# A sparse-attention stage whose index scores move from VectorE to TensorE

## The chip, the cores and the metric

The kernel runs on one core of one Trainium2 chip. The metric is the device time of one execution in microseconds; of several executions the median counts. TensorE (PE) multiplies matrices, VectorE (DVE), ScalarE (ACT) and GpSimd (POOL) work on tiles, SyncE (SP) issues most of the DMA transfers. Each engine works through its own list of instructions in the order in which the program wrote them, and waits on semaphores for the others.

## The reference

The program is two transformer blocks; the change lies in one stage of the second, the sparse attention (`dsa_attention`). For 512 tokens with 1,024 features, a small index network scores every earlier token for every token (8 index heads of 64 features), the best 128 are kept, and 16 heads of latent attention run over those alone. Cut to what matters:

```
h = x @ w_in                                   # 456 columns: c_q 256, c_kv 128, k_idx 64, w_idx 8
c_q, c_kv = rms_norm(c_q, g), rms_norm(c_kv, g)
q_idx = (c_q @ w_qidx).reshape(S, 8, 64)
k_idx = layer_norm(k_idx, g, b)
s_idx = einsum('thd,sd->ths', q_idx, k_idx)
score = einsum('ths,th->ts', relu(s_idx), w_idx * scale)     # sum over 8 index heads
score = where(key_pos <= t_pos, score, -inf)
_, sel = top_k(score, 128)
logits = einsum('thc,tkc->thk', q_abs, c_kv[sel]) * qk_scale + bias[t5_bucket(dist)]
o = softmax(logits) @ c_kv[sel] @ w_uv @ w_o
```

## The kernel before

Weights are float32. `WStream` loads them in slabs of 128 x 2048 and splits each into a high part (`wh`, a cast on ACT, L295) and a low part (`wl`, a subtraction on DVE or POOL, L302); a product is then three matmuls (`mm3`: high times high, L307, and the two mixed ones, L308 and L309). `ws.get()` hands out the next slab and splits so many further ones as `ws.ahead` says.

The stage is `dsa_in` (L2487), then `dsa_att`. No scheduler moves anything: the order of the calls is the order on every engine. Tokens come in four tiles of 128. `dsa_in` does the following.

- For each tile t, `gemm_n` makes the 512 columns of `x @ w_in` (24 matmuls, two slabs). For t = 0 and 1, `flip` turns the input tile that is needed two steps later (`xth`, `xtl`).
- `norm(t)` copies the result (`hs`, ACT), squares it for the norms, and after its first `yield` scales it (8 small DVE instructions with three square roots on ACT between them). `wi` holds the head weights.
- `turn(t)` transposes `hs` on PE (L2538), applies the gains (`df`, 4 DVE instructions) and splits into `ch` (ACT) and `cl` (DVE).
- `index_q(w, half)` makes the index queries of two tiles (24 matmuls of 256 columns, `xth`), `value` the attention values of a tile.
- `scores(i)` makes the scores of the rows of tile i against the 128 (i + 1) keys up to it: for each of 8 heads three matmuls, a Relu on ACT (L2567), and on DVE a multiplication by the head's weight that is added to `sco` (L2569, L2571); at the end a minimum with the causal mask (L2574). Tile 0 needs no selection.
- `select()` is a generator of DVE instructions. For one tile it takes 16 rounds, each a MAX (L2587: the eight largest) and a MATCH_REPLACE (L2589: strike them out), then an `is_equal` and a scaling into the mask `negm`. It runs tile 1, with tile 2 beside it once that is scored, and then tile 3. `step(n)` advances it by n steps; `scores(i, n)` takes n steps after each head.
- `make(h)` projects queries and keys of attention head h (9 matmuls, 2 ACT and 2 DVE instructions). Three heads are made ahead, with 8 steps after each; then the attention loop starts. It goes over heads for tiles 0 to 2 first, projects three heads ahead, and takes on the average 2.25 steps of the selection of tile 3 per iteration until that is done.

`dsa_in` sets `ws.lo_eng = "pool"` at its start, so that POOL makes the low parts. Before it, two constants are made on DVE: `identb` (L2473) and `negm[0]` (L2501).

Of the kernel before, what the change touches and what calls it, by code (L numbers as in the profile page):

```python
# [9 lines left out]
F32 = mybir.dt.float32  # L10
# [3 lines left out]
AF = mybir.ActivationFunctionType  # L14
OP = mybir.AluOpType
# [8 lines left out]
KT = D // 128  # L24
# [252 lines left out]
class Builder:  # L277
# [40 lines left out]
            if between and k % 2:  # L318
                between()

    def gemm_n(self, slabs, xh, xl, t0, ps):

        kk = 0
        n = 4 * len(slabs)
        for s in slabs:
            h = s[0].rearrange("p (k c) -> p k c", k=4)
            l = s[1].rearrange("p (k c) -> p k c", k=4)
            for k in range(4):
                self.mm3(ps, (xh[:, kk, t0:t0 + 128], xl[:, kk, t0:t0 + 128]), (h[:, k], l[:, k]), kk == 0, kk == n - 1)
                kk += 1  # L330
# [2131 lines left out]
    def phase_dsa(self):  # L2462
        nc, A, ws = self.nc, self.A, self.ws
        V, G, S_ = nc.vector, nc.gpsimd, nc.scalar
        dt = self.dram.tile
        self.d_dq = dt([16, 128, 2, 128], F32, name="d_dq")
        self.d_dk = dt([16, 128, 512], F32, name="d_dk")
        with ExitStack() as c:
            op_ = c.enter_context(self.pool(name="da_o", bufs=1))
            vs = op_.tile([128, 4, 1024], F32, name="vs")  # L2470
            negm = [op_.tile([128, 128 * (i + 1)], BF16, name=f"negm{i}") for i in range(4)]
            identb = op_.tile([128, 128], BF16, name="identb")
            V.tensor_copy(identb, self.ident)  # L2473
            with ExitStack() as c1:
                with ExitStack() as c2:
                    self.acc_pool(c2)
                    bg, load = self.dsa_in(c1, vs, negm, c2.enter_context(self.pool(name="da_pt", bufs=4, space=PSUM)))
                self.dsa_att(c1, vs, negm, identb, load, bg)
            self.acc_pool(c, 8)
            self.ln_gains(c, 2)  # L2480
            ws.ahead = 0
            self.last_gemm(lambda k, t: (self.xth[:, k, t * 128:(t + 1) * 128], self.xtl[:, k, t * 128:(t + 1) * 128]),
                           [ws.get() for _ in range(4)], KT, self.acc, "acc", DN_ALPHA)
            ws.ahead = 2
            ws.hi_eng, ws.lo_eng = "act", "dve"

    def dsa_in(self, c, vs, negm, pt):  # L2487

        nc, A, ws = self.nc, self.A, self.ws
# [8 lines left out]
        caus = vs[:, 3, 256:384]  # L2498
        nc.scalar.dma_start(out=caus, in_=A["causal"][:, 0:128])
        nc.scalar.dma_start(out=wrk[0][:, 0:128], in_=A["causal"][:, 128:256])  # L2500
        V.tensor_scalar(negm[0], wrk[0][:, 0:128], -1.0, None, op0=OP.mult)  # L2501
        sp = c.enter_context(self.pool(name="da_s", bufs=1))
        c1 = ExitStack()
        tp = c1.enter_context(self.pool(name="da_t", bufs=3))
# [11 lines left out]
        def norm(t, ps):  # L2516
            h, s = hs[t], ss[:, t]
            S_.copy(h, ps)
            S_.activation(jk, ps[:, 0:256], AF.Square, accum_out=s[:, 0:1], scale=1.0 / 16)
            S_.activation(jk[:, 0:128], ps[:, 256:384], AF.Square, accum_out=s[:, 1:2])  # L2520
            yield
            V.bn_stats(st[:, t], h[:, 384:448])
            V.bn_aggr(s[:, 6:8], st[:, t])
            V.tensor_scalar(wi[:, t], h[:, 448:456], 8 ** -0.5 * 64 ** -0.5, None, op0=OP.mult)
            S_.activation(s[:, 2:3], s[:, 0:1], AF.Sqrt, bias=self.eps_col(1e-6), scale=1.0)
            S_.activation(s[:, 3:4], s[:, 1:2], AF.Sqrt, bias=self.eps_col(1e-6), scale=1.0 / 128)
            S_.activation(s[:, 4:5], s[:, 7:8], AF.Sqrt, bias=self.eps_col(1e-5), scale=1.0)
            V.reciprocal(s[:, 2:5], s[:, 2:5])
            V.tensor_scalar(h[:, 448:512], h[:, 384:448], s[:, 6:7], s[:, 4:5], op0=OP.subtract, op1=OP.mult)
            V.tensor_scalar(h[:, 384:448], h[:, 384:448], s[:, 6:7], s[:, 4:5], op0=OP.subtract, op1=OP.mult)  # L2530
            V.tensor_scalar(h[:, 256:384], h[:, 256:384], s[:, 3:4], None, op0=OP.mult)
            V.tensor_scalar(h[:, 0:256], h[:, 0:256], s[:, 2:3], None, op0=OP.mult)
            yield
# [12 lines left out]
        def index_q(w, half):  # L2546
            e = slice(256 * half, 256 * half + 256)
            for j in range(4):
                ps = acc()
                for k in range(2):  # L2550
                    cs = slice(k * 512 + j * 128, k * 512 + j * 128 + 128)
                    self.mm3(ps[:, 0:256], (w[0][:, cs], w[1][:, cs]), (ch[:, k, e], cl[:, k, e]), k == 0, k == 1)
                self.split(ps[:, 0:256], iqh[:, j, e], iql[:, j, e])

        def step(n):
            for _ in range(n):
                next(bg, None)

        def scores(i, steps=0):
            n = 128 * (i + 1)  # L2560
            sc = ip.tile([128, n], F32, name=f"sco{i}")
            for h in range(8):
                j, r = h // 2, slice(64 * (h % 2), 64 * (h % 2) + 64)
                ps = acc()
                self.mm3(ps[:, 0:n], (iqh[r, j, tsl[i]], iql[r, j, tsl[i]]), (ch[r, 3, 0:n], cl[r, 3, 0:n]), True, True)
                f = tp.tile([128, 512], F32, name="df", tag="df")
                S_.activation(f[:, 0:n], ps[:, 0:n], AF.Relu)  # L2567
                if h == 0:
                    V.tensor_scalar(sc, f[:, 0:n], wi[:, i, h:h + 1], None, op0=OP.mult)  # L2569
                else:  # L2570
                    V.scalar_tensor_tensor(sc, f[:, 0:n], wi[:, i, h:h + 1], sc, op0=OP.mult, op1=OP.add)  # L2571
                step(steps)
                yield
            V.tensor_tensor(sc[:, n - 128:], sc[:, n - 128:], caus, op=OP.min)  # L2574
            sco[i] = sc

        ready = []
# [1 line left out]
        def select():  # L2579

            started = []

            def rounds(i):
                n, a = 128 * (i + 1), i % 2
                src, wk = sco[i], wrk[a if i < 3 else 0][:, 0:n]
                for r in range(16):
                    V.max(m8[:, a], src)  # L2587
                    yield
                    V.match_replace(wk, m8[:, a], src, -3.3e38)  # L2589
                    src = wk  # L2590
                    yield
                V.tensor_tensor(wk, wk, sco[i], op=OP.is_equal)
                yield
                V.tensor_scalar(negm[i], wk, 1.0e30, None, op0=OP.mult)
                ready.append(i)
            both = [rounds(1)]
            while both:
                for g in list(both):
                    if next(g, both) is both:
                        both.remove(g)  # L2600
                if sco[2] is not None and not started:
                    started.append(rounds(2))
                    both += started
                yield
            yield from rounds(3)

        def value(w, t):
            for half in range(2):
                ps = acc()
                cs = slice(1024 + half * 512, 1536 + half * 512)  # L2610
                self.mm3(ps, (ch[:, 2, tsl[t]], cl[:, 2, tsl[t]]), (w[0][:, cs], w[1][:, cs]), True, True)
                S_.copy(vs[:, t, half * 512:(half + 1) * 512], ps)
# [40 lines left out]
        def make(h):  # L2653
            made[h] = proj(h)

        ws.lo_eng = "pool"
        slabs = [ws.get(), ws.get()]
        for t in range(4):
            ps = acc()
            self.gemm_n(slabs, self.xth, self.xtl, t * 128, ps)  # L2660
            if t < 2:
                self.flip(t + 2, pt, "dpt")
            if t == 2:
                turn(0)
                turn(1)
                ws.ahead = 1
                wq = ws.get()
            nm = norm(t, ps)
            next(nm)
            if t < 3:  # L2670
                next(nm)
        index_q(wq, 0)
        turn(2)
        next(nm)
        value(wq, 0)
        for _ in scores(1):
            pass
        bg = select()
        turn(3)
        for t in range(1, 3):  # L2680
            value(wq, t)
            step(3)
        ws.ahead = 0
        wk = ws.get()
        c2.close()
        qp = c.enter_context(self.pool(name="db_q", bufs=3, side="right"))
        index_q(wq, 1)
        for _ in scores(2, 1):
            pass
        wu = [ws.get(), ws.get()]  # L2690
        for _ in scores(3, 4):
            pass
        for h in range(3):
            make(h)
            step(8)
# [132 lines left out]
```

## Time and profile before

| | |
|---|---|
| median of 3 executions | 3916.84 us (3914.33 to 3918.34) |
| profiled execution | 3919.22 us, span 3917.4 us |
| mean granted TensorE clock | 0.975 of full speed |
| busy share of the span | PE 95%, DVE 60%, ACT 38%, POOL 25% |
| chain that ended last | PE 76%, DVE 11%, DMA 6%, ACT 3% |

The span is the time from the first to the last instruction of the profiled execution, whose own time is 1.8 us longer. PE is busy for 95% of it, and where it isn't, another engine is late. In the 40 slices of the page, PE falls below nine tenths only in few; one of them is the stage above, which begins in the trace at 3259.55 us and hands over to the attention loop at about 3378 us. Such a stage is read from its own waits, not from the shares of the whole.

### The profile page before, as it was taken

Reading aid. Unit: us, or ns where it says so; the run is one execution under the profiler, and the core shown is the slowest. Engines: PE = TensorE matmul, PEld = TensorE weight load, DVE = VectorE, ACT = ScalarE, POOL = GpSimd, SP = SyncE. Lnnn points to the kernel's source line nnn. Section 1 sums busy time; section 2 is a strip of 40 time slices with the busy share of each in tenths; the row PEclk is TensorE's granted clock in tenths of the full one; section 3 lists DMA queues with packets and bytes.
Section 4 is the critical chain, followed back from the end, with each engine's and each line's share of the span. In section 5 each row is a group of like instructions: output and inputs, shape, how many; then the busy total and the mean of one; then the engine's idle time right before and its main releaser. Section 6 shows DMA issues by size and latency. Waiting matters only on the chain.

```text
span 3917.4 us, 49840 instructions
## 1 busy us (share of the span) xinstructions
PE 3709.7 (95%) x19451; PEld 3039.8 (78%) x19456; DVE 2330.9 (60%) x4013; ACT 1499.9 (38%) x2159; POOL 997.5 (25%) x574
## 2 busy tenths in 40 slices
PE   8999799999999999999999998898889998699999
PEld 4788667788888878888888886787778886588887
DVE  3564265596999963444434437783665548846455
ACT  3322275553544543322322324663333324443232
POOL 1201053325433431211211214752421001112010
PEclk9999899999999999999999999999999999799999
DMA  6374554324455566655655643469735222252221
GB/s 250 124 277 160 161 152 144 110 76 131 176 178 178 184 198 174 164 147 157 160 148 160 164 129 110 143 179 268 190 119 155 85 96 77 83 185 97 97 105 57
DMA packets 483964, 582.32 MB, mean 149 GB/s; under 512 B 337904, under 2 KB 379760, under 8 KB 446096
## 3 DMA queue, kind: packets, MB, share of 16 engines
q1 hardware_dynamic: 479552, 571.20, 47.9%
q10 hardware_dynamic: 4176, 7.93, 0.6%
q8 instruction: 153, 2.51, 0.3%
q14 instruction: 83, 0.68, 0.1%
HBM read 456.37 MB, written 121.63 MB: 148 GB/s over the span
## 4 chain that ended last, share of the span: by engine, by line
PE 76%; DVE 11%; DMA 6%; ACT 3%; POOL 2%; issue 2%; SPq 1%; ACTq 0%; DVEq 0%; POOLq 0%
PE acc L307 14%; PE acc L309 13%; PE acc L308 13%; PE pv L309 8%; PE pv L308 8%; PE pv L307 8%; PE psc L1520 3%; DMA d_k<-ql 1%; DMA d_q<-ql 1%; PE dpo L2760 1%; POOL wl L302 1%; PE pz L2071 1%; DVE ob L1532 1%; PE acc L644 1%; DVE st L961 1%
## 5 line engine op out<-in xcount | busy, mean ns | idle before, releaser
L295 ACT CAST wh<-wr 128x2048 fp32r<-128x2048 f32 (+2 forms) x310 | 510.2, 1664 | 398.0 <-PE pv L309 291.7
L302 DVE TENSOR_TENSOR wl<-wr,wh 128x2048 fp32r<-128x2048 f32 (+2 forms) x203 | 461.2, 2291 | 154.5 <-ACT wh L295 154.3
L307 PE MATMUL pv<-wh,ah 128*128 128x512 f32 x1376 | 538.0, 391 | 9.7 <-ACT wh L295 9.7
L308 PE MATMUL pv<-wl,ah 128*128 128x512 f32 x1376 | 537.0, 390 | 1.5 <-DVE wl L302 1.5
L309 PE MATMUL pv<-wh,al 128*128 128x512 f32 x1376 | 537.1, 390 | 0.0
L302 POOL TENSOR_TENSOR wl<-wr,wh 128x2048 fp32r<-128x2048 f32 (+1 forms) x113 | 387.3, 3440 | 540.7 <-ACT wh L295 505.7
L307 PE MATMUL acc<-h2h,wh 128*128 128x512 f32 x1024 | 412.9, 403 | 0.0
L309 PE MATMUL acc<-h2h,wl 128*128 128x512 f32 x1024 | 402.9, 393 | 0.0
L308 PE MATMUL acc<-h2l,wh 128*128 128x512 f32 x1024 | 399.2, 390 | 0.0
L307 PEld LDWEIGHTS pv<-wh,ah 128*128 128x128 f32 x1376 | 259.4, 188 | 64.1 <-ACT wh L295 10.2
L308 PEld LDWEIGHTS pv<-wl,ah 128*128 128x128 f32 x1376 | 259.1, 188 | 56.2 <-DVE wl L302 2.0
L309 PEld LDWEIGHTS pv<-wh,al 128*128 128x128 f32 x1376 | 259.1, 188 | 54.6
L307 PE MATMUL acc<-xth,wh 128*128 128x512 f32 (+1 forms) x768 | 287.4, 374 | 0.7 <-ACT xth L295 0.7
L309 PE MATMUL acc<-xth,wl 128*128 128x512 f32 (+1 forms) x768 | 286.8, 373 | 0.0
L308 PE MATMUL acc<-xtl,wh 128*128 128x512 f32 (+1 forms) x768 | 284.8, 371 | 1.1 <-DVE xtl L302 1.1
L1371 DVE TENSOR_TENSOR py<-py,pv 128x512 f32<-128x512 f32 x119 | 80.4, 685 | 323.7 <-PE pv L309 323.7
L1532 DVE TENSOR_SCALAR ob<-iota,ttt 128x128 f32<-128x128 f32 x512 | 238.3, 527 | 0.0
L309 PEld LDWEIGHTS acc<-h2h,wl 128*128 128x128 f32 x1024 | 192.1, 188 | 43.2
L1521 ACT COPY gs<-psc 128x512 f32<-128x512 f32 x128 | 143.4, 1120 | 210.5 <-PE psc L1520 207.2
L308 PEld LDWEIGHTS acc<-h2l,wh 128*128 128x128 f32 x1024 | 192.9, 188 | 38.6
L307 PEld LDWEIGHTS acc<-h2h,wh 128*128 128x128 f32 x1024 | 192.9, 188 | 35.3
L302 POOL TENSOR_TENSOR al<-cv,ah 128x512 fp32r<-128x512 f32 x44 | 57.0, 1296 | 632.4 <-ACT ah L295 569.6
(606 smaller groups left out, 7353.9 us busy)
## 6 DMA issues: line engine op xcount, KB each, us to landing
wr<-in_pu SPq DMA_DIRECT2D x64, 1024.0 KB
wr<-in_pv SPq DMA_DIRECT2D x64, 1024.0 KB
wr<-in_f_up SPq DMA_DIRECT2D x44, 1024.0 KB
d_g<-gs SPq DMA_DIRECT2D x16, 2048.0 KB
gt<-d_g SPq DMA_DIRECT2D x128, 256.0 KB
d_h<-he SPq DMA_DIRECT2D x84, 256.0 KB
hs<-d_h SPq DMA_DIRECT2D x84, 256.0 KB
wadb<-in_ada_b SPq DMA_DIRECT2D x32, 512.0 KB
```

The lines of the kernel that those rows point to most:

```text
L295: nc.scalar.copy(hi, src)
L302: (nc.vector if le == "dve" else nc.gpsimd).tensor_tensor(lo, src, hi.bitcast(F32), op=OP.subtract)
L307: mm(ps, w[0], x[0], start=first, stop=False)
L308: mm(ps, w[0], x[1], start=False, stop=False)
L309: mm(ps, w[1], x[0], start=False, stop=last)
L644: nc.tensor.matmul(ps[0:2], sc[:, 4 * half + k], w[:, k], start=(half + k == 0), stop=(half == 1 and k == 3))
L961: nc.vector.tensor_reduce(st[i][:, 2 + j:3 + j], ps[i, j], axis=AX.X, op=OP.max, negate=True)
L1371: nc.vector.tensor_tensor(yt, yt, ps, op=OP.add)
L1520: nc.tensor.matmul(pg[:, r], ob[:, r], oa[:, r], start=True, stop=True)
L1521: nc.scalar.copy(gs[:, :, q % 8 * 4:q % 8 * 4 + 4].rearrange("p i t -> p t i"), pg)
L1532: V.tensor_scalar(ob[:, r], iota, tt[:, 1, k + r:k + r + 1], tt[:, 2, k + r:k + r + 1], op0=OP.is_equal, op1=OP.mult)
L2071: nc.tensor.matmul(p[rows[hp], j], l[:, j, h64], r[:, j, h64] if r.shape[2] == 128 else r[:, j], start=True, stop=True)
```

## The change

Four things change in `dsa_in`.

1. `scores` no longer sums over heads on DVE. ACT first multiplies the identity by each head's column of weights, which gives 8 diagonal matrices (`dg`, new L2565, 128 x 128). PE then multiplies each by the head's Relu output and adds the products up in one PSUM tile (`total`, new L2577; both operands are plain float32). ACT copies the columns before the diagonal block, DVE takes the minimum for that block alone (new L2580, L2581).
2. `identb` and `negm[0]` are made on ACT.
3. Weight slabs are split when they are asked for and not ahead (`ws.ahead = 0`). The first (`wq`) keeps its low part on DVE and is split after the turning of tiles 0 and 1. The matmuls of tile 3 are cut into their two slabs (new arguments of `gemm_n`), with `index_q` between them.
4. The scores of tile 1 and the start of the selection come before the second half of `norm(2)` and `norm(3)`. The numbers of steps between the parts change: 8 before the scores of tile 2, 1 per head there (10 in all), 2 per head for tile 3 (20 in all), then 8 after each of the three projections as before.

```diff
-    def gemm_n(self, slabs, xh, xl, t0, ps):
-
-        kk = 0
-        n = 4 * len(slabs)
+    def gemm_n(self, slabs, xh, xl, t0, ps, k0=0, last=True):
+
+        kk = k0
+        n = k0 + 4 * len(slabs) if last else KT + 1
...
-            V.tensor_copy(identb, self.ident)
+            S_.copy(identb, self.ident)
...
-        V.tensor_scalar(negm[0], wrk[0][:, 0:128], -1.0, None, op0=OP.mult)
+        S_.mul(negm[0], wrk[0][:, 0:128], -1.0)
...
             sc = ip.tile([128, n], F32, name=f"sco{i}")
+            dg = vs[:, 2].rearrange("p (h c) -> p h c", c=128)
             for h in range(8):
-                j, r = h // 2, slice(64 * (h % 2), 64 * (h % 2) + 64)
-                ps = acc()
-                self.mm3(ps[:, 0:n], (iqh[r, j, tsl[i]], iql[r, j, tsl[i]]), (ch[r, 3, 0:n], cl[r, 3, 0:n]), True, True)
-                f = tp.tile([128, 512], F32, name="df", tag="df")
-                S_.activation(f[:, 0:n], ps[:, 0:n], AF.Relu)
-                if h == 0:
-                    V.tensor_scalar(sc, f[:, 0:n], wi[:, i, h:h + 1], None, op0=OP.mult)
-                else:
-                    V.scalar_tensor_tensor(sc, f[:, 0:n], wi[:, i, h:h + 1], sc, op0=OP.mult, op1=OP.add)
+                S_.mul(dg[:, h], self.ident, wi[:, i, h:h + 1])
+            total = pt.tile([128, 4, 128], F32, name="dpt", tag="dpt").rearrange("p a t -> p (a t)")
+            fs = []
+            for h in range(8 + 2):
+                if h < 8:
+                    j, r = h // 2, slice(64 * (h % 2), 64 * (h % 2) + 64)
+                    ps = acc()
+                    self.mm3(ps[:, 0:n], (iqh[r, j, tsl[i]], iql[r, j, tsl[i]]), (ch[r, 3, 0:n], cl[r, 3, 0:n]), True, True)
+                    f = tp.tile([128, 512], F32, name="df", tag="df")
+                    S_.activation(f[:, 0:n], ps[:, 0:n], AF.Relu)
+                    fs.append(f)
+                if h > 1:
+                    nc.tensor.matmul(total[:, 0:n], dg[:, h - 2], fs[h - 2][:, 0:n], start=(h == 2), stop=(h == 9))
                 step(steps)
-                yield
-            V.tensor_tensor(sc[:, n - 128:], sc[:, n - 128:], caus, op=OP.min)
+            if n > 128:
+                S_.copy(sc[:, 0:n - 128], total[:, 0:n - 128])
+            V.tensor_tensor(sc[:, n - 128:], total[:, n - 128:n], caus, op=OP.min)
...
-        ws.lo_eng = "pool"
+        bg = iter(())
+        ws.ahead = 0
         slabs = [ws.get(), ws.get()]
+        nms = []
         for t in range(4):
             ps = acc()
-            self.gemm_n(slabs, self.xth, self.xtl, t * 128, ps)
+            if t == 3:
+                ws.pump(ws.ng + 1)
+                self.gemm_n(slabs[:1], self.xth, self.xtl, t * 128, ps, last=False)
+                wq = ws.get()
+                index_q(wq, 0)
+                self.gemm_n(slabs[1:], self.xth, self.xtl, t * 128, ps, k0=4)
+            else:
+                self.gemm_n(slabs, self.xth, self.xtl, t * 128, ps)
             if t < 2:
                 self.flip(t + 2, pt, "dpt")
+            nm = norm(t, ps)
+            nms.append(nm)
+            next(nm)
+            if t < 2:
+                next(nm)
             if t == 2:
                 turn(0)
                 turn(1)
-                ws.ahead = 1
-                wq = ws.get()
-            nm = norm(t, ps)
-            next(nm)
-            if t < 3:
-                next(nm)
-        index_q(wq, 0)
+        scores(1)
+        bg = select()
+        ws.lo_eng = "pool"
+        next(nms[2])
         turn(2)
-        next(nm)
+        next(nms[3])
+        step(2)
         value(wq, 0)
-        for _ in scores(1):
-            pass
-        bg = select()
+        step(2)
         turn(3)
-        for t in range(1, 3):
-            value(wq, t)
-            step(3)
-        ws.ahead = 0
+        step(2)
+        value(wq, 1)
+        step(2)
+        index_q(wq, 1)
         wk = ws.get()
...
-        index_q(wq, 1)
-        for _ in scores(2, 1):
-            pass
+        scores(2, 1)
         wu = [ws.get(), ws.get()]
-        for _ in scores(3, 4):
-            pass
+        scores(3, 2)
+        value(wq, 2)
```

On DVE, between the turning of tile 1 (`cl`) and the norm of tile 2 (`hs_24416`), three entries are new: the low part of `wq` (`wl`), the low parts of the index queries (`xth`), and the minimum that ends the scores of tile 1 (`sco`).

```order
 L302 TENSOR_TENSOR cl<-df,ch 128x4x128
+L302 TENSOR_TENSOR wl<-wr,wh 128x2048
+L302 TENSOR_TENSOR xth<-acc,xth 128x256 x4
+L2581 TENSOR_TENSOR sco_24649<-dpt,vs 128x128
 L2522 BN_STATS dst<-hs_24416 128x6
```

The norm of tile 2, the turning of tile 2 and the norm of tile 3 now stand behind them in the list.

Further down on DVE, behind the norm of tile 3 (`hs_24417`) and ahead of the turning of tile 3 (`df`), the nine instructions that summed the scores of tile 1 are gone and the first two rounds of its selection stand there.

```order
 L2532 TENSOR_SCALAR hs_24417<-hs_24417,dss 128x256
-L2569 TENSOR_SCALAR sco_24699<-df,wi 128x256
-L2571 SCALAR_TENSOR_TENSOR sco_24699<-df,wi,sco_24699 128x256 x7
-L2574 TENSOR_TENSOR sco_24699<-sco_24699,vs 128x128
+L2594 MAX m_24398<-sco_24649 128x8
+L2596 MATCH_REPLACE vs<-m_24398,sco_24649 128x256
+L2594 MAX m_24398<-vs 128x8
+L2596 MATCH_REPLACE vs<-m_24398,vs 128x256
 L2540 TENSOR_SCALAR df<-dpt,cols 128x128
```

So the selection starts ahead of the turning of tile 3 and behind both norms.

On ACT, from the index queries of tiles 2 and 3 (`xth`) to the Relus of tile 3 (`df` of 512 columns), the list before is this; `wh` is a weight cast.

```order
L295 CAST xth<-acc 128x256 x4
L2567 ACTIVATE df<-acc 128x384 x8
L295 CAST wh<-wr 128x2048 x2
L2567 ACTIVATE df<-acc 128x512 x8
```

And this is the list now; `vs<-ident,wi` are the diagonal matrices, `sco` the copies out of `total`.

```order
L295 CAST xth<-acc 128x256 x4
L295 CAST wh<-wr 128x2048
L2565 ACTIVATE vs<-ident,wi 128x128 x8
L2574 ACTIVATE df<-acc 128x384 x8
L2580 COPY sco_24837<-dpt 128x256
L295 CAST wh<-wr 128x2048 x2
L2565 ACTIVATE vs<-ident,wi 128x128 x8
L2574 ACTIVATE df<-acc 128x512 x8
L2580 COPY sco_24927<-dpt 128x384
```

Ahead of each block of Relus there are now weight casts and eight multiplications, and all of them stand in the same list as the Relus.

## Rows read from the trace of the kernel before

**Rows 1.** Stretches: length, busy us of PE, PEld, DVE, ACT, POOL, clock, DMA.

```profile
3300.00:3310.00 10.00, 9.02 (x52) 7.71 (x53) 8.41 (x24) 6.22 (x16) 0.00 (x0) 0.83 0.00 0
3320.00:3330.00 10.00, 3.79 (x11) 2.80 (x12) 9.97 (x9) 2.75 (x5) 8.04 (x2) 0.57 0.40 123
3400.00:3405.00 5.00, 5.00 (x36) 4.33 (x35) 4.18 (x13) 3.11 (x9) 4.00 (x1) 1.00 0.39 118
```

**Rows 2.** Timeline of POOL; columns: start, duration, instruction, idle before and releaser.

```profile
3268.07 9.39 POOL L302 TENSOR_TENSOR wl<-wr,wh 128x2048 fp32r<-128x2048 f32 x2 [36.08 <-ACT wh L295]
```

**Rows 3.** Timeline of DVE beside POOL's two splits.

```profile
3268.45 4.64 DVE L2473 CAST identb<-ident 128x128 bf16<-128x128 f32 x1
...
3319.46 4.22 DVE L2574 TENSOR_TENSOR sco<-sco,vs 128x128 f32<-128x128 f32 x1
```

**Rows 4.** Timeline of PE, from tile 2 to the first scores.

```profile
3272.64 0.48 PE L307 MATMUL acc<-wh,xth 128*128 128x512 f32 x1
...
3278.20 0.80 PE L309 MATMUL acc<-wh,xtl 128*128 128x512 f32 x1 [4.85 <-DVE xtl L302]
...
3285.96 1.04 PE L2538 MATMUL dpt<-ident,hs 128*128 128x128 f32 x8
3286.75 0.48 PE L307 MATMUL acc<-wh,xth 128*128 128x512 f32 x1
...
3292.44 0.28 PE L307 MATMUL acc<-ch,wh 128*128 128x256 f32 x1
...
3295.17 0.60 PE L2538 MATMUL dpt<-ident,hs 128*128 128x128 f32 x4
...
3299.88 0.38 PE L307 MATMUL acc<-ch,xth 64*128 64x256 f32 x1 [2.15 <-ACT vs L2612]
```

**Rows 5.** Timeline of DVE: turning, a norm, first selection.

```profile
3288.47 0.69 DVE L302 TENSOR_TENSOR cl<-df,ch 128x512 fp32r<-128x512 f32 x1 [0.69 <-ACT ch L295]
...
3290.95 0.69 DVE L302 TENSOR_TENSOR cl<-df,ch 128x512 fp32r<-128x512 f32 x1 [0.69 <-ACT ch L295]
...
3298.59 0.22 DVE L2522 BATCH_NORM_STATS2 dst<-hs 128x6 f32<-128x64 f32 x1
...
3300.38 0.35 DVE L2532 TENSOR_SCALAR hs<-hs,dss 128x256 f32<-128x256 f32 x1
...
3307.82 0.42 DVE L2587 MAX8 m<-sco 128x8 f32<-128x256 f32 x1
...
3308.80 0.43 DVE L2587 MAX8 m<-vs 128x8 f32<-128x256 f32 x1
```

**Rows 6.** The page's groups; columns: shapes, count, busy us, mean ns, idle before.

```profile
L302 DVE TENSOR_TENSOR wl<-wr,wh 128x2048 fp32r<-128x2048 f32 (+2 forms) x203 | 461.2, 2291 | 154.5 <-ACT wh L295 154.3
```

**Rows 7.** Timeline of ACT.

```profile
3312.01 2.38 ACT L2567 ACTIVATE df<-acc 128x384 f32<-128x384 f32 x5 [0.75 <-PE acc L309]
...
3316.99 3.69 ACT L295 CAST wh<-wr 128x2048 fp32r<-128x2048 f32 x2
...
3378.87 0.40 ACT L2741 ACTIVATE dp<-dp,dsm 128x128 f32<-128x128 f32 x1 [0.42 <-DVE dsm L2733]
3379.18 0.19 ACT L2741 ACTIVATION_READ_ACCUMULATOR dp<-dp,dsm 128x1 f32 x1
```

**Rows 8.** Timeline of PE in the first block: plain float32 operands.

```profile
520.35 2.74 PE L1004 MATMUL pav<-at,av 128*128 128x512 f32 x6
```

**Rows 9.** Timeline of DVE: both selections, then that of tile 3.

```profile
3333.64 0.41 DVE L2587 MAX8 m<-vs 128x8 f32<-128x256 f32 x1
...
3335.35 0.74 DVE L2571 SCALAR_TENSOR_TENSOR sco<-df,wi,sco 128x512 f32<-128x512 f32 x1
...
3359.68 0.69 DVE L2587 MAX8 m<-sco 128x8 f32<-128x512 f32 x1
...
3378.54 0.29 DVE L2733 CUSTOM_DVE_ANT_0 dp<-acc,db 128x128 f32<-128x128 f32 x1
```

**Rows 10.** Instructions that write the scores; durations min/median/max in ns.

```profile
L2571 DVE SCALAR_TENSOR_TENSOR sco<-df,wi,sco x21: 483/600/739, 3301.1 to 3353.5; 128x256 f32<-128x256 f32 x7, 128x384 f32<-128x384 f32 x7, 128x512 f32<-128x512 f32 x7
```

## The prediction

> **What bounds the kernel now.** I read the shares first: PE is busy 95% of the span, so the change can only act where PE waits. The slices show such a place in the stage that the change rewrites, and its windows tell two parts apart [rows 1]. In 3300:3310 all engines work a little and the granted clock is 0.83; in 3320:3330 DVE is full (9.97 of 10 us) while PE has 3.79 us of work. In the attention loop behind it (3400:3405) PE is full at clock 1.00. I then followed the timelines of PE, DVE, ACT and POOL from 3259.55 to 3378.54, DVE's first instruction of the attention loop [rows 9]; what the change is worth is how far that handover moves.
>
> Early in the stage PE once waits 4.85 us for `xtl`, in the matmuls of tile 2 [rows 4]. DVE was late because casting the 128 x 128 `identb` took 4.64 us [rows 3], beside the two low parts on POOL that took 9.39 us [rows 2]; a scaling of twice that size takes DVE 0.35 [rows 5]. The min of the scores of tile 2 had the same fate (4.22 us, [rows 3]). From 3307.82, the first MAX, DVE is what ends last.
>
> **The change, step by step.** I carry two ends along one chain, "full" (PE starts each piece at full clock) and "low" (after each wait it starts at half, as the 0.83 of [rows 1] shows that it can). Full is written first.
>
> 1. `identb` and `negm[0]` leave DVE and POOL has no split there, so the 4.85 us wait goes. Tile 2 starts at 3272.64 [rows 4] and has 24 matmuls of 512 columns; 24 of them take 3292.44 − 3286.75, or 0.237 each, hence 5.7. The transposes of tiles 0 and 1 start at 3278.3 instead of 3285.96.
> 2. What is late next is `wq`. Two turnings take 3290.95 + 0.69 − 3285.96 = 5.7 [rows 4, 5], to 3284.0. ACT casts `wh` behind the second `ch` (from about 3283.3, 1.85 us, [rows 7]), to 3285.2; DVE's `wl` takes 2.29 [rows 6], to 3287.5. PE has the first slab of tile 3 meanwhile (2.8 us, to 3281.9) and then idles more than 5 us: most of the wait that was removed returns here.
> 3. Index queries, 24 matmuls at (3295.17 − 3292.44)/24 = 0.114 [rows 4]: 2.7, at half clock 5.5. End 3290.2 / 3293.0. The second slab of tile 3, 2.8: 3293.0 / 3295.8.
> 4. ACT must then copy and square tile 3 (1.3, estimated from 0.48 per Relu of 384 columns in [rows 7]) and make eight `dg`. A 128 x 128 ACT instruction with such an operand takes 0.40 and the next starts 0.31 later [rows 7]. Below, I bound it by 0.26: 1.85 for 2048 columns and 0.48 for 384 leave 0.16 us and 0.82 ns a column. I take 0.31, the nearer row: 2.5. With the first Relu 0.4: 3297.2 / 3300.0.
> 5. A product with plain float32 operands: six such matmul instructions of 512 columns take 2.74 us [rows 8], less the 0.15 by which a matmul's 0.39 exceeds its 0.237 [rows 4], so 0.43 each. Two instructions make one product: 0.86 for 512 columns, 0.65 for 384, 0.43 for 256. Tile 1: 8 × 0.43 + 15 × 0.114 = 5.2; the min is no longer beside a split, 0.5. Low adds 1.7, what ten microseconds at 0.83 lose to the half level twice over: 3302.9 / 3307.4.
> 6. Now DVE: the second halves of two norms (2 × (3300.38 + 0.35 − 3298.59) = 4.3) and one turning (3289.16 − 3285.96 = 3.2) [rows 4, 5] stand in its list between min and first MAX. First MAX at 3310.4 / 3314.9; before it was 3307.82. The selection that is written earlier starts later.
> 7. Two rounds of 0.98 and the turning of tile 3 (3290.95 − 3288.47 = 2.5) [rows 5], index queries 2.7 / 5.5, last cast and subtraction 0.8: 3318.3 / 3325.6.
> 8. Cast of `wk` 1.85, `dg` 2.5, Relu 0.5, of which 0.4 overlaps; tile 2 on PE 8 × 0.65 + 15 × 0.17 = 7.8, min 0.5, low again 1.7: 3331.0 / 3340.0.
> 9. ACT: copy 0.4, the two casts of `wu` 3.7 [rows 7], `dg` 2.5, Relu 0.6. PE: 8 × 0.86 + 15 × 0.237 = 10.4, min 0.5: 3349.1 / 3359.8. DVE's own steps there, 16 on both tiles at (3335.35 − 3333.64)/2 = 0.855 [rows 9] and 4 on tile 2 alone, are 16.2 us and end beside this.
> 10. Values of tile 2 and first projection, 12 × 0.237, and `qh` 0.8: 3352.7 / 3363.4.
> 11. DVE has 14 steps of tile 2 at 0.62 (halfway between 0.49, half a round of 256 columns [rows 5], and the next), and ten of tile 3 with six projection instructions at (3378.54 − 3359.68)/25 = 0.754 (first and last of 25 instructions, [rows 9]): 8.7 + 12.1 = 20.8. Handover at 3373.5 / 3384.2 against 3378.54: −5.0 / +5.7. The stage will have both levels, as now, so I take near the middle, +0.3.
> 12. Tile 3 had 21 steps done at the handover and will have 10. Eleven steps of 0.754 are 8.3 us more for DVE in the attention loop. Bounds 0 and 8.3; PE is full there while DVE, stepping, is 4.18 of 5 busy [rows 1], so I take 0.5.
>
> So DVE loses its 24 score sums (21 at a median of 0.6, [rows 10]) and the stalls of 4 us, and the stage still ends when it did: half the waits are now PE's for ACT and `wq`, and 11 steps have been put off. The sum is +0.8 on the profiled execution's 3919.22 (span 3917.4 and 1.8 around it), 3920.0. That execution lies 2.4 above the median, so the median goes to 3917.6.
>
> On step 4, the Trainium skill ("ScalarE: Activation LUTs", section "What ACT_TABLE_LOAD costs") gives an ACT instruction with one per-partition operand about 280 ns plus 0.833 a column, and says that one overlaps the next by 93 ns. By it 128 columns would be an estimated 387 ns and 294 apart; the row has 0.40 and 0.31, so the trace agrees, and the 24 `dg` would cost 7.1 us for my 7.4.
>
> **The rivals.**
> - Low clock after every wait. Three phases then begin on a PE that has just waited 5 to 10 us for a split or for ACT; for it speaks 0.57 in 3320:3330 [rows 1], against it that the matmuls of tile 2 returned to 0.39 us apiece soon after the 4.85 us wait [rows 4]. All low ends: 3916.84 + 5.7 + 0.5 = 3923.0. The Trainium skill ("TensorE: Matmul & The Clock Gate", section "HAM oscillation — how this bites in real kernels") describes this pattern, bursts between waits that each start slow, as a cost in itself; 0.57 agrees, and by that rule this rival would be the forecast.
> - Full clock throughout, with `dg` at 0.26 (24 × 0.05 = 1.2): 3916.84 − 5.0 − 1.2 + 0.5 = 3911.1. For it: PE has 15.5 us more of its own work, 8 × (0.43 + 0.65 + 0.86), and that fills its waits.
> - DVE stays the bound, and PE and ACT keep up behind their lists. From the middle first MAX, 3312.6, DVE alone needs 18 solo steps at 0.49, 8.8, the turning 2.5, subtractions 1.4, 16.2, 20.8 and 0.6: 50.3, so 3362.9, 15.6 earlier, and with 0.5 behind it 3901.7. It is what a count of DVE's work gives. Against it: steps 7 to 9 keep ACT's casts and `dg` ahead of every Relu, and only two or eight steps are there to bridge them.
> - Slower: the postponed steps come out in the attention loop. The price is 8.3 + 0.3, 3925.4. It decides where an iteration's DVE work with 2.25 steps exceeds PE's; 4.18 of 5 is against it, the 4.00 us of POOL in the same 5 us [rows 1] for it, since DVE's small operations took over 4 us beside POOL's long ones [rows 3].
> - That the selection isn't ahead in time is no rival but part of the forecast (step 6).
>
> **How the numbers follow.** Forecast 0.50, low clock 0.16, full clock 0.14, DVE the bound 0.10, slower 0.10. A measurement of this kernel tells some 0.2%, 7.8 us, from no change. Faster by more: DVE's case 0.10, a little under half of full clock's 0.06, and 0.02 of the forecast's: 0.18. Slower by more: 0.10, and 0.04 from the upper edge of the low clock: 0.14. The rest, 0.68, is the same. The likeliest case's own range is 3911 to 3923. For eight in ten I go from 3903, just above DVE's case, to 3926, above the slower one.
>
> **What would show it.** Right if the matmuls of tile 2 have no wait at about 3278 and the transposes start there; PE idles about 5 us before the index queries, released by `wl`; `dg` starts 0.3 apart and the sum's instructions 0.43; the first MAX comes at 3310 to 3315; and the handover between 3373 and 3384, with PE full in the attention loop. Wrong if the first MAX is well before 3307 (steps 2 to 6), if PE stops waiting from 3320 on (steps 8, 9), if new splits of POOL stretch DVE's or ACT's small instructions to 4 us, or if DVE ends attention iterations (step 12).

## The result, and the profile after

The changed kernel takes 3942.57 us (median of 4, 3941.06 to 3943.95), 1.0063 of the time before (95% interval 1.0051 to 1.0075): some 25 us slower, where 3917.6 and a range of 3903 to 3926 were forecast. The profiled execution took 3942.84 us, span 3941.1, for 3919.22 and 3917.4.

All of it lies in the stage. From the first matmul of `x @ w_in` to DVE's first instruction of the attention loop it took 3378.54 − 3259.78 = 118.8 us; now 3403.90 − 3259.28 = 144.6. Three stretches of the kernel after, one in each of the three score phases (columns: length, busy us of PE, PEld, DVE, ACT, POOL, granted clock, DMA), which answer to [rows 1]:

```profile
3300.00:3310.00 10.00, 10.00 (x26) 6.06 (x25) 0.00 (x0) 1.92 (x5) 0.00 (x0) 0.50 0.00 0
3335.00:3350.00 15.00, 15.00 (x27) 7.23 (x27) 0.00 (x0) 2.46 (x5) 0.39 (x1) 0.50 0.21 71
3360.00:3375.00 15.00, 15.00 (x23) 5.89 (x23) 7.27 (x23) 2.39 (x4) 2.41 (x1) 0.50 0.34 126
```

PE, which had 3.79 of 10 us to do in 3320:3330 before, is now busy without a break in all three, at clock 0.50, which is the lower of its two levels (1.2 of 2.4 GHz). DVE, which was full, has nothing to do in two of them. The bound has changed over to PE, and PE runs at half speed.

The early part came nearly as forecast. PE's timeline after, against [rows 4] (x2 at a product counts its two instructions):

```profile
3277.83 1.04 PE L2538 MATMUL dpt<-ident,hs 128*128 128x128 f32 x8
...
3284.70 0.38 PE L307 MATMUL acc<-ch,wh 128*128 128x256 f32 x1 [3.04 <-ACT wh L295]
...
3287.03 0.58 PE L309 MATMUL acc<-ch,wl 128*128 128x256 f32 x1 [1.83 <-DVE wl L302]
...
3298.08 1.22 PE L2577 MATMUL dpt<-df,vs 128*128 128x256 f32 x2 [3.15 <-ACT df L2574]
```

The 4.85 us wait is gone, and 3.04 + 1.83 us of waiting for `wq` stand in its place. Then the first two products of tile 2, and the phase of tile 3, with its wait, a head, the start of the next, and the last three products:

```profile
3333.54 0.91 PE L2577 MATMUL dpt<-df,vs 128*128 128x384 f32 x2 [3.72 <-ACT df L2574]
...
3335.55 1.65 PE L2577 MATMUL dpt<-df,vs 128*128 128x384 f32 x2
...
3357.98 2.08 PE L2577 MATMUL dpt<-df,vs 128*128 128x512 f32 x2 [5.06 <-ACT df L2574]
3359.99 0.79 PE L307 MATMUL acc<-ch,xth 64*128 64x512 f32 x1
3360.58 0.62 PE L308 MATMUL acc<-cl,xth 64*128 64x512 f32 x1
3361.01 0.62 PE L309 MATMUL acc<-ch,xth 64*128 64x512 f32 x1
3361.56 2.07 PE L2577 MATMUL dpt<-df,vs 128*128 128x512 f32 x2
...
3375.88 4.31 PE L2577 MATMUL dpt<-df,vs 128*128 128x512 f32 x6
```

In tile 2 the first product behind the wait took 0.91 and was still at full clock, and the next took 1.65. In tile 3 one product takes 2.01 us (3357.98 to 3359.99) where 0.86 was forecast, one head 3.58. Only the last three products, which follow each other, get faster (3.75 us to the next matmul at 3379.63, for three times 2.01). ACT's list shows why PE waited:

```profile
3351.40 3.70 ACT L295 CAST wh<-wr 128x2048 fp32r<-128x2048 f32 x2
3355.00 2.45 ACT L2565 ACTIVATE vs<-ident,wi 128x128 f32<-128x128 f32 x8
3357.35 1.54 ACT L2574 ACTIVATE df<-acc 128x512 f32<-128x512 f32 x3
```

DVE's timeline after: the three minima, the first MAX, the handover (against [rows 5, 9]).

```profile
3311.78 0.29 DVE L2581 TENSOR_TENSOR sco<-dpt,vs 128x128 f32<-128x128 f32 x1 [19.66 <-ACT sco L2580]
...
3319.46 0.42 DVE L2594 MAX8 m<-sco 128x8 f32<-128x256 f32 x1
...
3351.53 0.29 DVE L2581 TENSOR_TENSOR sco<-dpt,vs 128x128 f32<-128x128 f32 x1 [17.31 <-ACT sco L2580]
...
3380.75 0.29 DVE L2581 TENSOR_TENSOR sco<-dpt,vs 128x128 f32<-128x128 f32 x1 [13.34 <-ACT sco L2580]
...
3403.90 0.29 DVE L2748 CUSTOM_DVE_ANT_0 dp<-acc,db 128x128 f32<-128x128 f32 x1
```

DVE idles 19.66, 17.31 and 13.34 us for the sums that were taken off it. Its first MAX comes behind the norms of tiles 2 and 3: the scores of tile 1 were moved ahead of them, the selection's first step was not.

### The profile page after: what moved, and what is told of

It is laid out like the page before. It is cut to its first block, busy times and chain, and to the rows that moved or that the text cites. A ratio compares the mean times of both kernels' runs of the same rounds, so it can differ in the third digit from the quotient of the medians.

```text
span 3941.1 us, 49927 instructions
## 1 busy us (share of the span) xinstructions
PE 3749.3 (95%) x19499; PEld 3056.4 (78%) x19504; DVE 2307.5 (59%) x3988; ACT 1509.6 (38%) x2188; POOL 991.8 (25%) x573
## 4 chain that ended last, share of the span: by engine, by line
PE 77%; DVE 10%; DMA 6%; ACT 3%; POOL 2%; issue 2%; SPq 1%; ACTq 0%; DVEq 0%; POOLq 0%
PE acc L307 14%; PE acc L309 14%; PE acc L308 13%; PE pv L308 8%; PE pv L307 8%; PE pv L309 8%; PE psc L1520 3%; DMA d_k<-ql 1%; DMA d_q<-ql 1%; PE dpt L2577 1%; POOL wl L302 1%; PE pz L2071 1%; DVE ob L1532 1%; PE acc L644 1%; PE dpo L2775 1%
```

## The experiments

Theory A: the float32 products lost the time, since they hold PE at its lower level. Theory B: the new order did. Theory C, and out of it D after the first runs: the waits ahead of the phases bring the clock down, and the alternation of products and score matmuls doesn't bring it back. In the table, fp32r is the rounded format of the casts (`wh`, `ch`); a product on it is one instruction and not two. All ratios are to the kernel before on the same chip; "stage" is read from the profile as above.

| run | ratio (95%) | stage, us |
|---|---|---|
| before / after | 1 / 1.0063 (1.0051 to 1.0075) | 118.8 / 144.6 |
| e1: after, sums on DVE | 1.0006 (0.9997 to 1.0015) | 119.0 |
| e2: before, sums on PE alone | 1.0038 (1.0023 to 1.0052) | 131.4 |
| e3: before, two casts on ACT alone | 0.9997 (0.9988 to 1.0005) | 116.9 |
| e4: after, fp32r products | 1.0018 (1.0009 to 1.0027) | 122.3 |
| e5: after, products grouped | 1.0000 (0.9991 to 1.0009) | 117.9 |
| e6: after, no waits ahead | 0.9977 (0.9968 to 0.9986) | 108.4 |
| e7: e6 with fewer steps | 0.9972 (0.9962 to 0.9982) | 102.9 |
| e8: e6 with one wait back | 1.0007 (0.9997 to 1.0016) | 120.7 |
| e9: e7 with norms in the shadow | 0.9965 (0.9952 to 0.9978) | 99.6 |
| e10: e9 with 8 steps | 0.9972 (0.9962 to 0.9981) | 105.2 |
| e11: e9 with slabs together | 0.9956 (0.9942 to 0.9970) | 95.5 |

**e1.** In `scores`, the old sum in the new order.

```diff
-                    nc.tensor.matmul(total[:, 0:n], dg[:, h - 2], fs[h - 2][:, 0:n], start=(h == 2), stop=(h == 9))
+                        V.scalar_tensor_tensor(sc, f[:, 0:n], wi[:, i, h:h + 1], sc, op0=OP.mult, op1=OP.add)
```

> The changed kernel, with the sum over heads put back on VectorE (no diagonal matrices, no float32 products); order, splits, step counts and the two casts on ScalarE stay changed. Theory A: the 25 us were lost in the float32 products, which keep TensorE at its lower level of 1.2 GHz while they alternate with the score matmuls (2.01 us for 512 columns where I had 0.86). Without them the time is near that of before, 3912 to 3922. Theory B: the loss lies in the new order (norms and turnings between the scores of tile 1 and the first MAX, first MAX at 3319 for 3308, weight casts ahead of the Relus, 11 steps put off). Then only the 7.4 us of the diagonal matrices come back: 3930 to 3938.

Measured 3919.99, the time of before. With the sums on DVE, order, splits and postponed steps cost nothing that can be measured, so B alone falls. That the sums on PE cost all of it holds for this order of ScalarE's list; e6 changes that list and finds no cost.

**e2.** The kernel before with the new sums (and `value(wq, 2)` behind `scores(3)`).

> The kernel before, with the sums over heads as diagonal matmuls alone (the values of tile 2 come after the scores of tile 3, because the diagonal matrices lie in their place); order, splits and step counts of before. Theory A: slower by 15 to 30, 3933 to 3948, with the granted clock at 0.50 in the three phases. Theory B: the sums leave VectorE, which bounds this stage, and nothing else moves: 3905 to 3919.

Measured 3934.51, inside A's range but slower by 15, not by 25, and its stretches show a difference that A can't explain. The phase of tile 2 and that of tile 3:

```profile
3327.00:3335.00 8.00, 8.00 (x27) 4.15 (x27) 1.08 (x4) 2.47 (x6) 0.00 (x0) 1.00 0.01 2
3350.00:3365.00 15.00, 15.00 (x22) 5.78 (x21) 10.67 (x30) 2.39 (x4) 0.00 (x0) 0.50 0.12 50
```

The same kind of instructions ran at 1.00 in one phase, behind a wait of 1.46 us, and at 0.50 in the other, behind 5.29 us. In tile 1, behind 2.47 us, a product took the 1.22 us of half clock.

```profile
3303.37 1.22 PE L2576 MATMUL dpt<-df,vs 128*128 128x256 f32 x2 [2.47 <-ACT df L2573]
...
3326.31 0.91 PE L2576 MATMUL dpt<-df,vs 128*128 128x384 f32 x2 [1.46 <-ACT df L2573]
...
3343.23 2.08 PE L2576 MATMUL dpt<-df,vs 128*128 128x512 f32 x2 [5.29 <-ACT df L2573]
```

**e3.** `S_.copy(identb, self.ident)` and `S_.mul(negm[0], ...)` alone.

> The kernel before, with the two constants identb and negm[0] made on ScalarE and nothing else. Both theories: the 4.85 us wait of tile 2 for xtl goes, and everything up to the first MAX comes about 5 us earlier; VectorE bounds what follows and starts earlier by as much, so 3911 to 3914. If the wait was hidden behind later ones: 3916 to 3919.

Measured 3917.53 for 3919.56 on the same chip, the second of the two expectations; no difference can be claimed. The wait of 4.85 us is gone from its trace, but two others (1.07 and 2.44 us, for the norms) appear at the transposes, and the stage is 1.8 us shorter. The two stalls beside POOL's second split stay:

```profile
3319.03 4.22 DVE L2574 TENSOR_TENSOR sco<-sco,vs 128x128 f32<-128x128 f32 x1
3323.18 4.72 DVE L2569 TENSOR_SCALAR sco<-df,wi 128x512 f32<-128x512 f32 x1
```

**e4.** The operands of the products as fp32r.

```diff
-            dg = vs[:, 2].rearrange("p (h c) -> p h c", c=128)
+            dg = tp.tile([128, 8, 128], F32R, name="dgr", tag="dgr", bufs=1)
...
-                    f = tp.tile([128, 512], F32, name="df", tag="df")
+                    f = tp.tile([128, 512], F32R, name="dfr", tag="dfr")
```

> The changed kernel, with the products on operands rounded to fp32r, one pass each, in buffers of their own; what the rounding drops of the weights and of the Relus is left out. Theory A: the three phases run at the full clock like the matmuls beside them, 0.237 per 512-column product, and the handover to the attention loop comes near 3376: 3910 to 3920. Theory C: the waits before each phase alone set the clock, which then stays at 0.50 in the phases with these products too: 3920 to 3930 (tile 3: 8 x 4 x 0.43 = 13.8 us instead of 28.6, and VectorE's 16 us beside it). Theory B: 3930 or more.

Measured 3924.45, in C's range and outside A's. The phase of tile 2 is short but stays at half clock, although there is no float32 pass in it any more:

```profile
3329.00:3339.00 10.00, 10.00 (x26) 6.13 (x26) 0.94 (x4) 3.69 (x7) 0.41 (x1) 0.50 0.32 107
```

Its first two products show how it gets there: the first, behind the wait of 3.72 us, still runs at full clock, the second no longer.

```profile
3327.56 0.44 PE L2577 MATMUL dpt<-dfr,dgr 128*128 128x384 f32 x1 [3.72 <-ACT dfr L2574]
...
3328.69 0.69 PE L2577 MATMUL dpt<-dfr,dgr 128*128 128x384 f32 x1
```

So the format sets what a product costs at either level, not the level. A falls as I had put it. And a phase doesn't simply keep the level with which it begins, as e5, e6 and e8 put it below: in tile 2, here and in the kernel after, it begins at full clock and loses it within its first head.

**e5.** All eight products of a tile behind its score matmuls, eight Relu buffers.

```diff
-                if h > 1:
-                    nc.tensor.matmul(total[:, 0:n], dg[:, h - 2], fs[h - 2][:, 0:n], start=(h == 2), stop=(h == 9))
+            for h in range(8):
+                nc.tensor.matmul(total[:, 0:n], dg[:, h], fs[h][:, 0:n], start=(h == 0), stop=(h == 7))
```

> The changed kernel with the eight products of a tile behind all its score matmuls (eight buffers for the Relus instead of three), instead of one product after each head. Theory D: a phase that begins after a wait of 3 to 5 us begins at half clock, and it is the alternation of short score matmuls and products that doesn't bring it back, whatever the products' format; eight products in a row should then reach the full clock after two or three of them, as the last three of a tile seem to do now. Per tile about 8 x 1.3 us of score matmuls, three products at 1.0 to 2.0 and five at 0.43 to 0.86: some 3 to 5 us less per phase, 3928 to 3937. Theory A (float32 products hold the clock down themselves): 0.50 to the end of each phase, 3940 to 3946.

Measured 3918.85: D's direction, but 9 us beyond D's number. PE in tile 3:

```profile
3344.51 0.62 PE L307 MATMUL acc<-ch,xth 64*128 64x512 f32 x1
...
3345.92 8.41 PE L2578 MATMUL dpt<-df,vs 128*128 128x512 f32 x16
```

The score matmuls still ran at half clock (0.62 for the 0.39 of full); the eight products behind them took 3353.76 − 3345.92 = 7.84 us, 0.98 each, for 2.01. Behind the same kind of wait (5.28 us), float32 products in a row do bring the clock back, and the grouping alone restores the time of before. I had allowed three products at half clock; by the mean it was about one.

**e6.** Only ACT's list: diagonal matrices made ahead in two buffers, the casts of `wk` and `wu` between Relus.

```diff
-            for h in range(8):
-                S_.mul(dg[:, h], self.ident, wi[:, i, h:h + 1])
...
-        scores(2, 1)
-        wu = [ws.get(), ws.get()]
-        scores(3, 2)
+        scores(2, dg2, 1, {1: take, 3: lambda: diag(3, range(4), dg3), 5: lambda: diag(3, range(4, 8), dg3), 6: take})
+        scores(3, dg3, 2, {1: take})
```

> The changed kernel with ScalarE's list in another order and nothing else: the diagonal matrices are made ahead, in buffers of their own, and the casts of wk and wu lie between the Relus and not in front of them, so that TensorE doesn't wait 3 to 5 us ahead of each phase. Theory D (a phase keeps the clock with which it begins): the products start after 1 us or less, the phases of tiles 2 and 3 run at clock 1.00 (1.57 us per head of tile 2 as in the run of the sums alone, for 2.83), and the handover comes 20 to 28 us earlier: 3912 to 3923. Theory A (the products hold the clock down): only the waits go, some 10 us: 3930 to 3935.

Measured 3908.43, 34 us below the changed kernel and below even D's range, with the same instructions on PE. Of the three waits one is left (0.83 us, tile 1). The three phases:

```profile
3295.00:3301.00 6.00, 6.00 (x27) 3.92 (x28) 0.00 (x0) 1.92 (x5) 0.00 (x0) 1.00 0.00 0
3318.00:3328.00 10.00, 9.90 (x31) 4.82 (x31) 4.11 (x14) 8.76 (x18) 5.67 (x2) 1.00 0.23 66
3330.00:3342.00 12.00, 12.00 (x32) 4.92 (x31) 11.97 (x42) 5.39 (x8) 5.97 (x2) 1.00 0.53 175
```

and a head of tile 3, 1.95 us for 3.58:

```profile
3329.79 1.12 PE L2583 MATMUL dpt<-df,ddg 128*128 128x512 f32 x2
3330.85 0.49 PE L307 MATMUL acc<-ch,xth 64*128 64x512 f32 x1
...
3331.74 1.12 PE L2583 MATMUL dpt<-df,ddg 128*128 128x512 f32 x2
```

**e8.** e6 with the two casts of `wu` in front of `scores(3)` again.

> The run without waits, with the two casts of wu put back in front of the Relus of tile 3 and nothing else: one wait of some 3 to 4 us ahead of one phase. Theory D (a phase keeps the clock with which it begins): the phase of tile 3 runs at 0.50, 26 us for 13, and the time is 3918 to 3924, which is far more than the wait itself. Theory A or a plain wait: 3910 to 3913.

Measured 3920.49, 12 us more than e6 for one wait of 2.97 us; tile 2 kept 1.00, tile 3 fell:

```profile
3336.61 2.01 PE L2583 MATMUL dpt<-df,ddg 128*128 128x512 f32 x2 [2.97 <-ACT df L2578]
...
3340.11 2.07 PE L2583 MATMUL dpt<-df,ddg 128*128 128x512 f32 x2
```

This is what D forecast: the wait costs what it lasts, and then half the speed of what follows in the phase.

**e7, e9, e10, e11** go on from e6: `step(5)` for `step(8)` behind each projection (e7); the norms of tiles 2 and 3 inside the wait for tile 1's sums (e9); that with 8 steps (e10); and both slabs of tile 3 ahead of the index queries (e11).

> The run without waits (3908.4, 0.9977 of before), with 5 selection steps instead of 8 behind each of the three projections; tile 2's selection is still finished before the attention loop. Ten steps of tile 3 (0.75 us each) move into the attention loop. If the loop hides them as I took for the eleven steps of the change: 7.5 us earlier, 3899 to 3903. If they come out there (VectorE is 8.8 of 10 us busy in the loop's first iterations): 3907 to 3911.

> The run with fewer steps, and the second halves of the norms of tiles 2 and 3 put where VectorE now waits for the sums of tile 1 (behind the first index queries, and behind the sixth Relu), so ahead of the first selection. The first MAX follows the min at once and comes some 6 us earlier (3303 for 3309). If the path runs through the first MAX as in my steps 6 to 11: 5 to 7 us less than the run with fewer steps. If ScalarE's square roots between the Relus make TensorE wait and lose its clock in the phase of tile 1: no gain, or up to 5 us slower.

> The run with the norms in the shadow, with 8 steps behind each projection again; so the run without waits plus the norms alone. The stage (first matmul of x @ w_in to the handover) was 108.4 us without waits, 102.9 with fewer steps, 99.6 with both. If the postponed steps are lost again in the attention loop, as the 5.5 us shorter stage that gave only about 1 us suggests: stage near 105 and 3903 to 3907, the same as with 5 steps. If the loop hides them: 3908 to 3912.

> The run with the norms in the shadow (5 steps), with the two slabs of tile 3 together again ahead of the index queries, so that 2.8 us of matmuls lie in the wait for wq's casts, and ScalarE has copied tile 3 before the Relus of tile 1. If the wait for wq is on the path: the stage is 2 to 3 us shorter than 99.6 and the time 3900 to 3904. If not (tile 1's first product then waits longer on ScalarE): no change.

e7: 3907.46; the stage is 5.5 us shorter and the time only 1 to 2 us, inside the intervals. e9: 3904.55, the stage 3.3 shorter than e7, not 5 to 7. e10: 3906.89, stage 105.2; the norms alone shorten e6's stage by 3.2. The steps that 5 in place of 8 puts off (e7, e9) thus come out again for the most part in the attention loop (between e9 and e10 5.6 us of stage give 2 to 3 us of time, again inside the intervals). e11 is the fastest, 3899.22, with a stage 4.0 us shorter than e9's, more than forecast: the index queries start without PE's 3.04 us wait for `wh`, and take 0.28 us each where half of e9's took 0.41.

```profile
3288.14 0.39 PE L307 MATMUL acc<-ch,wh 128*128 128x256 f32 x1 [0.24 <-ACT wh L295]
```

## Why the prediction was wrong, step by step

| step | forecast, full / low | after |
|---|---|---|
| 1, transposes start | 3278.3 | 3277.83 |
| 2, PE idle for `wq` | over 5 | 4.9 |
| 4, first product | 3297.2 / 3300.0 | 3298.08 |
| 5, product to min of tile 1 | 5.7 / 7.4 | 14.0 |
| 6, min to first MAX | 7.5 | 7.4 |
| 7, to the last subtraction | 7.9 / 10.7 | 10.0 |
| 8, to the min of tile 2 | 12.7 / 14.4 | 22.4 |
| 9, to the min of tile 3 | 18.1 / 19.8 | 29.2 |
| 11, DVE to the handover | 20.8 | 20.3 |

Steps 1 to 4, 6, 7 and 11 held, and step 10 took 2.6 us for 3.6; `dg` took 2.43 to 2.45 us for eight (2.5 forecast). The steps that failed are 5, 8 and 9, in one term: "Low adds 1.7, what ten microseconds at 0.83 lose". I read the loss from a stretch in which the clock recovered [rows 1] and took it for the price of any wait. In these phases it doesn't recover until the last three products, and the three steps exceed even the low end by 6.6 + 8.0 + 9.4 = 24.0 us. By the low ends the handover would have come at 3384.2; it came at 3403.90, 19.7 later, since the other steps stayed 4.3 below theirs. e6 and e8 show the term. From the first product of a tile to its min (for tile 3, to the matmul behind the last product) the phases took 14.0, 18.3 and 21.7 us in the kernel after and 8.1, 10.8 and 12.0 in e6. So where the sum has 1.7 for each phase, the clock cost 5.9, 7.5 and 9.7: 23 us, beside the 11.9 us of waits ahead of them (3.15, 3.72, 5.06), of which e6 keeps 0.83. e8 loses 12 us again by one wait.

A smaller error lies in the product itself. At full clock it takes 1.06 us for 512 columns and 0.85 for 384 (e6, e2), 0.2 more than the 0.86 and 0.65 of step 5, and for 256 it takes 0.63 for 0.43: I took six products of one kind in a row [rows 8] for products that alternate with other matmuls. Over 24 products that is 5 us.

Step 12 held: the stage grew by 25.9 us and the span by 23.7, so the postponed steps cost nothing that shows there. They were twelve and not eleven: the kernel after has 9 steps of tile 3 behind it at the handover, for 21 before. Why the loop had room for these is not shown; DVE's 0.8 of 5 us that were left [rows 1] may be the reason. e7 put off nine more, and most of those came out.

Of the rivals, the low clock after every wait had the mechanism; it got 0.16 and 3923.0 because I priced it with the same 1.7. I had held against it that the matmuls of tile 2 recovered after their 4.85 us wait [rows 4]; those were 128-row matmuls of 512 columns in a row. The Trainium skill ("TensorE: Matmul & The Clock Gate", section "HAM oscillation — how this bites in real kernels") describes bursts that each start slow; the traces agree with it, and go further, since here a burst was still slow after 17.9 us (3357.98 to 3375.88) with PE busy throughout. "DVE stays the bound" was wrong from the first MAX on.

What stays open: why the level stays low in these phases. e4 rules out the float32 format, e5 the products as such. That the alternation does it, perhaps by small gaps that weight loads between unlike matmuls leave, is argued only. A rival stands beside it: the score matmuls themselves, which have 64 rows (64*128 in the listing, where the others have 128*128) and are part of every phase at half clock. In e1 no product stands between them, and behind a wait they too ran at half clock until they paused 5 us later; no run has a longer stretch of them:

```profile
3321.56 0.69 PE L307 MATMUL acc<-ch,xth 64*128 64x384 f32 x1 [3.45 <-ACT df L2569]
...
3326.13 0.62 PE L309 MATMUL acc<-ch,xth 64*128 64x512 f32 x1
```

## What to carry to other kernels

Moving work to an engine that idles is priced at the clock which that engine will have there: look for the longest wait ahead of the moved work, and price a whole phase at half speed if only short, mixed matmuls follow, as here. Before such a move, put what feeds it (here ScalarE's casts and diagonal matrices) in gaps instead of in front: that alone turned 1.0063 into 0.9977, and three small moves more into 0.9956. If the waits can't go, keep the moved matmuls in a row: e5 left a wait of 5.28 us, grouped the products and got to 1.0000. A recovery that the trace shows holds for the matmuls that made it, not for others.

## What the runs showed of the hardware that I had not expected

- The granted clock stayed at 0.50 for 15 us and more with PE busy 15.00 of 15.00 (kernel after, tiles 2 and 3), and at 1.00 for phases of the same build behind a shorter wait: 1.46 us (e2, tile 2) or none (e6, tiles 2 and 3), where the phases at 0.50 had waited 2.47 to 5.29 us.
- Beside POOL's split, DVE's min over `sco`, a scaling and a cast stretch to over 4 us (e3's two rows above, and [rows 3]), while MAX and MATCH_REPLACE don't. In the kernel after, DVE's rounds beside 9.03 us of POOL are as fast as ever:

```profile
3353.38 9.03 POOL L302 TENSOR_TENSOR wl<-wr,wh 128x2048 fp32r<-128x2048 f32 x2 [17.99 <-ACT wh L295]
...
3354.77 0.41 DVE L2594 MAX8 m<-vs 128x8 f32<-128x256 f32 x1
...
3355.68 0.41 DVE L2596 MATCH_REPLACE8 vs<-m,vs 128x256 f32<-128x256 f32 x1
```

- The new min, which reads `total` from PSUM and not `sco`, isn't stretched either. In e6 it lies beside a split and takes the 0.29 us that it takes alone:

```profile
3326.88 4.55 POOL L302 TENSOR_TENSOR wl<-wr,wh 128x2048 fp32r<-128x2048 f32 x1 [2.04 <-PE dpt L2583]
...
3328.60 0.29 DVE L2587 TENSOR_TENSOR sco<-dpt,vs 128x128 f32<-128x128 f32 x1 [6.21 <-ACT sco L2586]
```
